# Seven-product chunks on places 0, 2, 4, 6 and 1, 3, 5 in the late stages of a hybrid encoder layer

## The chip, the cores and the metric

One core of one Trainium2 chip. The metric is the device time of one execution in microseconds (us). The matrix engine is called PE or TensorE below, VectorE is DVE, ScalarE is ACT, GpSimd is POOL, and SyncE (SP) issues the transfers.

## The reference

A sequence of S = 256 tokens of width D = 2048 goes through one layer of two mixer branches (an mLSTM branch `ya` and an RG-LRU branch `yb`) in float32. The part that matters here is its end:

```python
ya = jnp.einsum('bsw,wd->bsd', ya, w_branch_a)
yb = jnp.einsum('bsw,wd->bsd', yb, w_branch_b)
merged = sigmoid(ga_p) * ya + sigmoid(gb_p) * yb      # ga_p, gb_p: columns of rms_norm(x) @ w_in
return x + jnp.einsum('bsd,de->bse', merged, w_out)   # then a last RMS norm
```

So there are five products of a 256 x 2048 matrix by a 2048 x 2048 weight matrix at the end: with w_branch_b, with the gate columns for b, with those for a, with w_branch_a, and with w_out.

## The kernel before, in words

Each float32 operand is split into a high and a low part in the matrix engine's reduced format, and a product is three matmuls: high by high (L174), high by low (L176), low by high (L177). Weights arrive in chunks of 256 rows of k by 512 columns (one tile `raw` of 128 x 1024, 512 KB, one transfer by SP). ScalarE casts the chunk to its high part `whi` and VectorE subtracts to get the low part `wlo` (L140, L141 in `load_chunk`). Activations (`sHL`, `sC`, `sD`, `sA`, `sB`) stay in SBUF, already split.

The late stages run in this order: WB (w_branch_b), GB (the gate for b), GA (the gate for a), WA (w_branch_a), WO (w_out). WB, GB, GA and WA each call `pair` twice. One `pair` makes two blocks of 512 columns over all of k, in eight chunks of k for each block. A chunk of both blocks is done in one of two ways:

- `plain`: a transfer, a cast and a subtraction for each block, then 12 matmuls for each block, 24 in all, into the block's accumulator `acc` in PSUM.
- `products`: a scheme with seven products on the 2 x 2 arrangement of half chunks, 21 matmuls. VectorE first makes sums of weight halves: t1 by L199 and L200, t2 by L203 and L204. ScalarE casts four pieces (L180: `b`, then three `whi`) and VectorE subtracts four times (L181: `b` on 512 columns, three `wlo` on 1024). Four of the seven products go to four single PSUM banks `aux` (p1, p5, p7, p6), three into the accumulators. The scheme needs a *form* of the activations, a stationary operand that `make_form` prepares beforehand: six VectorE operations (L277, L280 to L283, L285; two on 512 columns, four on 128; the first is left out where the sum exists already) and one cast (L284).

`kqs` names the chunks that are done by `products`, `places` the positions 0 to 7 in the pair's order at which these stand. After the last of them, ScalarE copies p1 (L252) and VectorE combines the four banks (L253 to L256). The chunks that are left are plain, first those of block 0, then those of block 1; behind each block VectorE adds its accumulator to the result (L262), which frees the accumulator for the next pair. Then an epilogue follows: in GB a sigmoid (L956) and a multiplication into the result (L957), in GA a sigmoid (L965).

There are two accumulators, so a pair's first matmul into one waits for the L262 of the pair before. `raw` has six buffers, `whi` and `wlo` four each; `b` alternates between two tiles. A scheduler sets the order of each engine's instructions when the program is built. It prefers what stands under `urgent()`; on the chip each engine then works strictly in that order. Forms of the normalised input (`h`) for chunks 0 and 4 exist since earlier stages, in the tiles F0 and F4; four slots of one tile PT hold others. The table of the weights on the host follows `kqs`, since a chunk done by `products` needs its halves of two blocks together.

Of the kernel before, what the change touches and what calls it, by code (L numbers as in the profile page):

```python
# [10 lines left out]
F32R = mybir.dt.float32r  # L11
# [8 lines left out]
NB = 512  # L20
# [3 lines left out]
EPS = 1e-6  # L24
NEG = -1e30

S_WB, S_GB, S_GA, S_WA = [((0, 2, 4), (0, 2, 4))] * 4
S_OZ = (((4, 0), (2, 4)), ((4,), (1,)), ((4, 0), (2, 5)), ((4, 0), (0, 2)))
S_V = (((4,), (4,)), ((4,), (4,)))
S_WO = (0, 1, 2, 4)  # L30
L_WB, L_GB, L_GA, L_WA = ((0, 2, 4), (0, 2, 4)), ((0, 2, 4), (0, 2, 4)), ((0, 2, 4), (0, 2, 4)), ((0, 2, 4), (1, 3, 5))
L_WO = (0, 2, 4, 6)
H_FORMS = (4, 0)
PLAN = (dict(Y=('c0', '', '', 'c1',),
# [12 lines left out]
def f(ap):  # L47
    return ap.bitcast(F32)
# [3 lines left out]
def hybrid_encoder(ctx: ExitStack, tc: tile.TileContext, x, xt, pk, bif, fg, wg, wi, wr, wa, wb, wo, out):  # L52
# [12 lines left out]
    def name(n):  # L65
        uid[0] += 1
        return f"{n}_{uid[0]}"
# [4 lines left out]
    def sl(tag, dt=F32, cols=4096):  # L72
        return slot.tile([P, cols], dt, tag=tag, name=name("s" + tag))
# [41 lines left out]
    def drain():  # L115
        while queue or any(lanes):
            tick()
        lanes.clear()
# [149 lines left out]
    def halves(t, i):  # L268
        return t[:, i * 1024:i * 1024 + NB], t[:, i * 1024 + NB:(i + 1) * 1024]

    def make_form(fm, full=None, parts=None, temp=None):
        u = xp.rearrange("p a b -> p (a b)") if temp is None else temp
        if full is None:
            full = u[:, NB:2 * NB]
            hi, lo = parts
            v = full if len(hi.shape) == 2 else full.rearrange("p (k s) -> p k s", s=S)
            dve.tensor_add(v, f(hi), f(lo))  # L277
        a11, a21, a12, a22 = [full[:, i * P:(i + 1) * P] for i in range(4)]
        s1, s2, s3, s4 = [u[:, i * P:(i + 1) * P] for i in range(4)]
        dve.tensor_add(s1, a21, a22)  # L280
        dve.tensor_sub(s2, s1, a11)
        dve.tensor_sub(s3, a11, a21)
        dve.tensor_sub(s4, a12, s2)  # L283
        act.copy(fm[0], u[:, :NB])  # L284
        dve.tensor_sub(fm[1], u[:, :NB], f(fm[0]))  # L285
# [20 lines left out]
    def half_tr(src, half, after=None, turn=False):  # L306
        ps, both = acc_pair()
        for kq in range(4):
            tick()
            hi, lo = load_chunk(src[half * 4 + kq])  # L310
            tiles = [(kq * 4 + kk, m, kk * S + m * P) for kk in range(4) for m in range(2)]
            for high in (False, True) if turn and kq % 2 else (True, False):
                for k, m, o in tiles:
                    if high:
                        pe.matmul(ps[m], hi[:, o:o + P], hl_t[:, 2 * k * S:2 * (k + 1) * S],  # L315
                                  start=(k == 0), stop=(turn and k == KT - 1), skip_group_check=True)
                    else:
                        pe.matmul(ps[m][:, :S], lo[:, o:o + P], hhi(k * S, (k + 1) * S),  # L318
                                  start=False, stop=(not turn and k == KT - 1), skip_group_check=True)
            if after:  # L320
                after(kq)
        return both.rearrange("p (m q s) -> p m q s", m=2, q=2)

    def fold(dst, both):
        t = hp.tile([P, NB], F32, tag="fold", name=name("fold"), bufs=1)
        t3 = t.rearrange("p (m s) -> p m s", m=2)
        with urgent():
            act.copy(t3, both[:, :, 1, :])
            d3 = dst if len(dst.shape) == 3 else dst.rearrange("p (m s) -> p m s", m=2)
            dve.tensor_add(d3, both[:, :, 0, :], t3)  # L330
        return dst
# [458 lines left out]
    def h_parts(kq):  # L790
        h4 = hl_t[:, kq * 4 * S:(kq + 1) * 4 * S].rearrange("p (k q s) -> p k q s", q=2, s=S)
        return [h4[:, :, q, :] for q in range(2)]
# [97 lines left out]
    yah, yal = Cols([yas["h"]], 4096), Cols([yas["l"]], 4096)  # L890
    ybh, ybl = [], []
    fslot = {}
    fm_t = []

    def form(x, kq, i, **kw):
        fslot[x, kq] = halves(fm_t[0], i)
        make_form(fslot[x, kq], **kw)

    def h_form(kq, i):
        form("h", kq, i, parts=h_parts(kq))  # L900

    def ya_form(kq, i):
        form("a", kq, i, parts=[t(kq * NB, (kq + 1) * NB) for t in (yah, yal)])

    def forms(x):
        return {kq: v for (n, kq), v in fslot.items() if n == x}
# [3 lines left out]

    k_yb, k_h, k_ya = (sorted(set(sum(v, ()))) for v in (S_WB, S_GB + S_GA, S_WA))
    k_h = [kq for kq in k_h if kq not in hf]
    early = [lambda kq=kq, i=i: h_form(kq, i) for kq, i in zip(k_h, (3, 0, 1))]
    early += [lambda kq=kq, i=i: ya_form(kq, i) for kq, i in zip(k_ya[:1], (3, 0, 1)[len(early):])]

    for j in range(4):
        for i in range(2):
            both = half_tr(wi[BLK_ZB + j], i)
            if i == 0:
                zt = hp.tile([P, 2 * NB], F32, tag="zz" if j else "vhi", name=name("zt"))  # L920
                sg = hp.tile([P, 2 * NB], F32, tag="to" if j else "vlo", name=name("sg"))
            fold(zt[:, i * NB:(i + 1) * NB], both)
        act.activation(sg, zt, AF.Silu)
        dve.tensor_mul(sg, sg, hs[:, j * 1024:(j + 1) * 1024])
        ybh.append(sl(f"C{j}", F32R, 1024))
        ybl.append(sl(f"D{j}", F32R, 1024))
        act.copy(ybh[j], sg)
        dve.tensor_sub(ybl[j], sg, f(ybh[j]))
        if j == 0:
            fm_t.append(sl("PT", F32R))  # L930
        if j == 0:
            drain()
        for kq in (2 * j, 2 * j + 1):
            if kq in k_yb:
                form("b", kq, k_yb.index(kq), full=sg[:, (kq % 2) * NB:(kq % 2 + 1) * NB])
        if j == 1:
            early[0]()
    ybh, ybl = Cols(ybh, 1024), Cols(ybl, 1024)
    nb11 = [0]

# [6 lines left out]
    sgv = [sgb[:, j * 1024:(j + 1) * 1024] for j in range(4)]  # L947
    for p in range(2):
        pair((wb[2 * p], wb[2 * p + 1]), ybh, ybl, forms("b"), S_WB[p], sgv[2 * p:2 * p + 2], b11, lambda jj: None, None, L_WB[p])
    for fn in early[1:]:  # L950
        fn()
    for p in range(2):
        gb = [sl(f"D{2 * p + i}", F32, 1024) for i in range(2)]

        def epi_gb(jj, p=p, gb=gb):
            act.activation(gb[jj], gb[jj], AF.Sigmoid)  # L956
            dve.tensor_mul(sgv[2 * p + jj], sgv[2 * p + jj], gb[jj])  # L957

        pair((wi[BLK_GB + 2 * p], wi[BLK_GB + 2 * p + 1]), hhi, hlo, forms("h"), S_GB[p], gb, b11, epi_gb, None, L_GB[p])
    ga = []  # L960
    for p in range(2):
        ga += [sl(f"C{2 * p + i}", F32, 1024) for i in range(2)]
# [2 lines left out]
            act.activation(ga[2 * p + jj], ga[2 * p + jj], AF.Sigmoid)  # L965

        pair((wi[BLK_GA + 2 * p], wi[BLK_GA + 2 * p + 1]), hhi, hlo, forms("h"), S_GA[p], ga[2 * p:], b11, epi_ga, None, L_GA[p])
    for i, kq in enumerate(k_ya[1:]):
        ya_form(kq, 1 + i)

    m_t = sl("HL", F32R, 8192)
    mh, ml = Cols([m_t[:, :4096]], 4096), Cols([m_t[:, 4096:]], 4096)
# [157 lines left out]
```

## Time and profile before

| | |
|---|---|
| median of three runs | 1013.25 us (1013.14 to 1013.77) |
| span of the profiled execution | 1012.2 us; the page gives no other time for it |
| PE busy | 1003.0 us, 99% of the span |
| VectorE busy | 875.8 us, 87% |
| ScalarE busy | 628.6 us, 62% |
| WB / GB / GA / WA | 583.8 to 668.0 / 751.0 / 834.2 / 917.2 us |

Times are microseconds from the start of the span; a row of the timeline gives start, duration, engine, line, operation, output and inputs, and in brackets the idle time ahead of it with what ended it. PEld is the loading of stationary operands, which runs beside the matmuls. A matmul's recorded 0.39 us overlaps with the next one's; what counts is the distance from start to start.

### The profile page before, as it was taken

Reading aid. Unit: us, or ns where it says so; the run is one execution under the profiler, and the core shown is the slowest. Engines: PE = TensorE matmul, PEld = TensorE weight load, DVE = VectorE, ACT = ScalarE, POOL = GpSimd, SP = SyncE. Lnnn points to the kernel's source line nnn. Section 1 sums busy time; section 2 is a strip of 40 time slices with the busy share of each in tenths; the row PEclk is TensorE's granted clock in tenths of the full one; section 3 lists DMA queues with packets and bytes.
Section 4 is the critical chain, followed back from the end, with each engine's and each line's share of the span. In section 5 each row is a group of like instructions: output and inputs, shape, how many; then the busy total and the mean of one; then the engine's idle time right before and its main releaser. Section 6 shows DMA issues by size and latency. Waiting matters only on the chain.

```text
span 1012.2 us, 13718 instructions
## 1 busy us (share of the span) xinstructions
PE 1003.0 (99%) x5045; PEld 853.2 (84%) x5045; DVE 875.8 (87%) x1167; ACT 628.6 (62%) x825; POOL 18.6 (2%) x37
## 2 busy tenths in 40 slices
PE   9999999999999999999999999999999999999997
PEld 9888988888888888888888888888888888888886
DVE  6687898889769888997697888998898988999996
ACT  7546477756695786667955564655655656455562
POOL 1000000001001000000100000000000000000000
PEclk9999999999999999999999999999999999999999
DMA  9765446565555565657466466666566656568452
GB/s 349 263 208 157 160 153 198 173 213 197 167 190 167 177 197 184 210 167 227 146 199 208 155 208 188 212 212 201 187 216 200 219 177 212 184 217 336 161 200 83
DMA packets 56387, 199.32 MB, mean 197 GB/s; under 512 B 6400, under 2 KB 7424, under 8 KB 55936
## 3 DMA queue, kind: packets, MB, share of 16 engines
q1 hardware_dynamic: 55456, 197.13, 58.9%
q10 hardware_dynamic: 864, 1.32, 0.4%
q8 instruction: 39, 0.64, 0.3%
q14 instruction: 28, 0.23, 0.1%
HBM read 196.33 MB, written 2.10 MB: 196 GB/s over the span
## 4 chain that ended last, share of the span: by engine, by line
PE 97%; DVE 1%; DMA 1%; ACT 0%; issue 0%; ACTq 0%; SPq 0%; DVEq 0%
PE acc L176 17%; PE acc L177 17%; PE acc L174 17%; PE acc L315 16%; PE acc L318 8%; PE aux L176 3%; PE aux L174 3%; PE aux L177 3%; PE aux L855 1%; PE aux L721 1%; PE aux L720 1%; PE aux L719 1%; PE aux L1053 1%; PE aux L1052 1%; PE aux L1051 1%; PE acc L156 1%
## 5 line engine op out<-in xcount | busy, mean ns | idle before, releaser
L140 ACT CAST whi<-raw 128x1024 fp32r<-128x1024 f32 (+1 forms) x284 | 294.8, 1046 | 196.0 <-PE acc L177 99.7
L141 DVE TENSOR_TENSOR wlo<-raw,whi 128x1024 fp32r<-128x1024 f32 (+1 forms) x284 | 341.5, 1213 | 76.2 <-ACT whi L140 74.4
L176 PE MATMUL acc<-wlo,sHL 128*128 128x512 f32 x554 | 215.9, 390 | 0.0
L177 PE MATMUL acc<-whi,sHL 128*128 128x512 f32 x554 | 215.8, 390 | 0.0
L174 PE MATMUL acc<-whi,sHL 128*128 128x512 f32 x554 | 213.3, 390 | 0.0
L315 PE MATMUL acc<-sHL,whi 128*128 128x512 f32 x704 | 175.9, 393 | 0.0
L315 PEld LDWEIGHTS acc<-sHL,whi 128*128 128x128 f32 x704 | 127.4, 189 | 23.5
L174 PEld LDWEIGHTS acc<-whi,sHL 128*128 128x128 f32 x554 | 104.0, 188 | 21.2
L176 PEld LDWEIGHTS acc<-wlo,sHL 128*128 128x128 f32 x554 | 104.1, 188 | 21.0
L177 PEld LDWEIGHTS acc<-whi,sHL 128*128 128x128 f32 x554 | 104.0, 188 | 20.9
L318 PEld LDWEIGHTS acc<-sHL,wlo 128*128 128x128 f32 x704 | 95.3, 190 | 6.0
L180 ACT CAST whi<-t 128x1024 fp32r<-128x1024 f32 x70 | 73.5, 1051 | 42.9 <-PE acc L177 13.9
L318 PE MATMUL acc<-sHL,wlo 128*128 128x256 f32 x704 | 99.0, 283 | 0.0
L181 DVE TENSOR_TENSOR wlo<-t,whi 128x1024 fp32r<-128x1024 f32 x70 | 85.5, 1222 | 9.0 <-ACT whi L180 8.5
L180 ACT CAST whi<-raw 128x1024 fp32r<-128x1024 f32 x37 | 39.0, 1053 | 27.6 <-PE acc L177 16.9
L181 DVE TENSOR_TENSOR wlo<-raw,whi 128x1024 fp32r<-128x1024 f32 x37 | 45.2, 1222 | 8.7 <-ACT whi L180 8.7
L180 ACT CAST b<-raw 128x512 fp32r<-128x512 f32 x28 | 17.4, 621 | 39.2 <-DMA raw<-wi 16.5
L176 PE MATMUL acc<-wlo,sC 128*128 128x512 f32 x92 | 35.9, 390 | 0.4 <-DVE wlo L141 0.4
L176 PE MATMUL acc<-wlo,sA 128*128 128x512 f32 x92 | 36.0, 392 | 0.0
L177 PE MATMUL acc<-whi,sD 128*128 128x512 f32 x92 | 35.8, 389 | 0.0
L177 PE MATMUL acc<-whi,sB 128*128 128x512 f32 x92 | 35.8, 389 | 0.0
L174 PE MATMUL acc<-whi,sC 128*128 128x512 f32 x92 | 35.3, 389 | 0.0
(361 smaller groups left out, 1589.1 us busy)
## 6 DMA issues: line engine op xcount, KB each, us to landing
raw<-wi SPq DMA_DIRECT2D x254, 512.0 KB, 4.2
raw<-wb SPq DMA_DIRECT2D x32, 512.0 KB, 4.1
raw<-wa SPq DMA_DIRECT2D x32, 512.0 KB, 4.0
raw<-wo SPq DMA_DIRECT2D x32, 512.0 KB, 4.8
raw<-wr SPq DMA_DIRECT2D x8, 512.0 KB, 4.0
sB<-x SPq DMA_DIRECT2D x4, 512.0 KB, 7.7
sA<-x SPq DMA_DIRECT2D x1, 2048.0 KB, 7.9
sA<-xt SPq DMA_DIRECT2D x7, 256.0 KB, 6.7
```

Source lines behind the costliest of these rows:

```text
L140: last_copy[0] = act.copy(hi[:, r], raw[:, r]).ins
L141: last_sub[0] = dve.tensor_sub(lo[:, r], raw[:, r], f(hi[:, r])).ins
L156: pe.matmul(ps[tb], a, wl, start=False, stop=False)
L174: pe.matmul(ps, a, wh, start=id(ps) not in began, stop=False)
L176: pe.matmul(ps, a, wl, start=False, stop=False)
L177: pe.matmul(ps, b, wh, start=False, stop=stop)
L180: act.copy(hi, v)
L181: dve.tensor_sub(lo, v, f(hi))
L315: pe.matmul(ps[m], hi[:, o:o + P], hl_t[:, 2 * k * S:2 * (k + 1) * S], start=(k == 0), stop=(turn and k == KT - 1), skip_group_check=True)
L318: pe.matmul(ps[m][:, :S], lo[:, o:o + P], hhi(k * S, (k + 1) * S), start=False, stop=(not turn and k == KT - 1), skip_group_check=True)
L719: pe.matmul(dst, whi[:, o:o + P], xh[:, r], start=True, stop=False)
L720: pe.matmul(dst, whi[:, o:o + P], xl[:, r], start=False, stop=False)
```

## The change

The first pair of each of the four stages does chunks 0, 2, 4 and 6 by `products`, on places 0, 2, 4, 6 (before: chunks 0, 2, 4 on these places). The second pair does three, on places 1, 3, 5; before, that was so in WA only, and on 0, 2, 4 in the other three stages. The forms that this needs: one more for b (chunk 6, in the slot that an early form of h had), two of h (chunks 2 and 6) built after WB into slots 0 and 1, and four of a: two built one after each pair of GB into slots 2 and 3, two built after GA into the tiles F0 and F4.

```diff
-S_WB, S_GB, S_GA, S_WA = [((0, 2, 4), (0, 2, 4))] * 4
+S_WB, S_GB, S_GA, S_WA = [((0, 2, 4, 6), (0, 2, 4))] * 4
...
-L_WB, L_GB, L_GA, L_WA = ((0, 2, 4), (0, 2, 4)), ((0, 2, 4), (0, 2, 4)), ((0, 2, 4), (0, 2, 4)), ((0, 2, 4), (1, 3, 5))
+L_WB, L_GB, L_GA, L_WA = [((0, 2, 4, 6), (1, 3, 5))] * 4
...
-    early = [lambda kq=kq, i=i: h_form(kq, i) for kq, i in zip(k_h, (3, 0, 1))]
-    early += [lambda kq=kq, i=i: ya_form(kq, i) for kq, i in zip(k_ya[:1], (3, 0, 1)[len(early):])]
...
-        if j == 1:
-            early[0]()
...
-    for fn in early[1:]:
-        fn()
+    for i, kq in enumerate(k_h):
+        h_form(kq, i)
...
         pair((wi[BLK_GB + 2 * p], ...), hhi, hlo, forms("h"), S_GB[p], gb, b11, epi_gb, None, L_GB[p])
+        ya_form(k_ya[p], 2 + p)
...
-    for i, kq in enumerate(k_ya[1:]):
-        ya_form(kq, 1 + i)
+    for kq, slot_ in zip(k_ya[2:], H_FORMS[::-1]):
+        fslot["a", kq] = halves(sl(f"F{slot_}", F32R, 1024), 0)
+        make_form(fslot["a", kq], parts=[t(kq * NB, (kq + 1) * NB) for t in (yah, yal)])
```

Later lines move up by three to five: the sigmoid of GB is L951 after the change and its multiplication L952, the sigmoid of GA L961. In the instruction counts PE goes from 5030 to 5018 rows (L174, L176 and L177 lose four each), VectorE from 1151 to 1192, ScalarE from 814 to 825; SP's transfers stay at 387.

Below are rows of the orders. A row gives the line, the operation, its output and its inputs, with buffer numbers. `t` are the sums of weight halves, `b11` is b, `sD0` and `sD1` hold the gate blocks, `aux` the four banks.

VectorE before the change, in GB between the first and the second pair, from the last combination of the banks (L256) to the first `wlo` of the second pair's first product chunk:

```order
L256 TENSOR_TENSOR sD1_1341_6228<-aux_1357_6257,sD0_1340_6227 128x512
L199 TENSOR_TENSOR t_1435_6575<-raw_1432_6568 128x512
L181 TENSOR_TENSOR b11_1434_6572<-raw_1432_6568,b11_1434_6572 128x512
L200 TENSOR_TENSOR t_1435_6575<-raw_1433_6569,raw_1432_6568 128x512
L141 TENSOR_TENSOR wlo_1421_6527<-raw_1419_6525,whi_1420_6526 128x1024
L141 TENSOR_TENSOR wlo_1425_6545<-raw_1423_6543,whi_1424_6544 128x1024
L203 TENSOR_TENSOR t_1436_6576<-t_1435_6575,raw_1432_6568 128x512
L262 TENSOR_TENSOR sD0_1340_6227<-sD0_1340_6227,acc_1342_6229 128x1024
L181 TENSOR_TENSOR wlo_1438_6580<-t_1435_6575,whi_1437_6579 128x1024
```

Two subtractions for plain chunks (L141) and the first accumulator's L262 stand among the work for the second pair, and three more plain chunks of each block come behind L253 on PE.

VectorE after the change, at the same turn, from the first combination (L253) to the second product chunk's `b`:

```order
L253 TENSOR_TENSOR sD1_1345_6244<-aux_1363_6275,sD0_1344_6243 128x512
L141 TENSOR_TENSOR wlo_1433_6571<-raw_1431_6569,whi_1432_6570 128x1024
L141 TENSOR_TENSOR wlo_1442_6603<-raw_1440_6601,whi_1441_6602 128x1024
L200 TENSOR_TENSOR t_1451_6644<-raw_1449_6638,raw_1448_6637 128x512
L254 TENSOR_TENSOR sD0_1344_6243<-aux_1362_6274,sD1_1345_6244 128x512
L141 TENSOR_TENSOR wlo_1446_6621<-raw_1444_6619,whi_1445_6620 128x1024
L203 TENSOR_TENSOR t_1452_6645<-t_1451_6644,raw_1448_6637 128x512
L255 TENSOR_TENSOR sD1_1345_6244<-aux_1361_6273,sD1_1345_6244 128x512
L256 TENSOR_TENSOR sD1_1345_6244<-aux_1361_6273,sD0_1344_6243 128x512
L181 TENSOR_TENSOR wlo_1454_6649<-t_1451_6644,whi_1453_6648 128x1024
L204 TENSOR_TENSOR t_1452_6645<-raw_1449_6638,t_1452_6645 128x512
L181 TENSOR_TENSOR b11_1474_6727<-raw_1472_6723,b11_1474_6727 128x512
```

The four combinations now alternate with the last plain chunk's subtractions (1433), with those of the second pair's place 0 (1442, 1446) and with the sums of its place 1 (L200, L203, L204). The rows that follow directly:

```order
L262 TENSOR_TENSOR sD0_1344_6243<-sD0_1344_6243,acc_1346_6245 128x1024
L262 TENSOR_TENSOR sD1_1345_6244<-sD1_1345_6244,acc_1347_6246 128x1024
L199 TENSOR_TENSOR t_1475_6730<-raw_1472_6723 128x512
L200 TENSOR_TENSOR t_1475_6730<-raw_1473_6724,raw_1472_6723 128x512
L181 TENSOR_TENSOR wlo_1456_6655<-t_1452_6645,whi_1455_6654 128x1024
L181 TENSOR_TENSOR wlo_1458_6659<-raw_1449_6638,whi_1457_6658 128x1024
L952 TENSOR_TENSOR sE_1169_5556<-sE_1169_5556,sD0_1344_6243 128x1024
L952 TENSOR_TENSOR sE_1169_5556<-sE_1169_5556,sD1_1345_6244 128x1024
L203 TENSOR_TENSOR t_1476_6731<-t_1475_6730,raw_1472_6723 128x512
L141 TENSOR_TENSOR wlo_1466_6689<-raw_1464_6687,whi_1465_6688 128x1024
```

Both L262 stand here, behind `wlo_1454` and `b11_1474`, and the two multiplications L952 stand ahead of `wlo_1466`, a plain chunk of the second pair.

PE after the change, at the same turn, beginning 35 rows behind the last matmul into p6 (`aux_1363`, which L253 reads); between them stand the rest of that product chunk, one plain chunk of each block and the second pair's first `b` product:

```order
L174 MATMUL aux_1461_6664<-whi_1453_6648,sF0_295_1520 128x512
L174 MATMUL aux_1459_6662<-b11_1474_6727,sHL_5_90 128x512
L174 MATMUL aux_1460_6663<-whi_1453_6648,sF0_295_1520 128x512
L176 MATMUL aux_1460_6663<-wlo_1454_6649,sF0_295_1520 128x512
L177 MATMUL aux_1460_6663<-whi_1453_6648,sF0_295_1520 128x512
L176 MATMUL aux_1461_6664<-wlo_1454_6649,sF0_295_1520 128x512
L177 MATMUL aux_1461_6664<-whi_1453_6648,sF0_295_1520 128x512
L176 MATMUL aux_1459_6662<-b11_1474_6727,sHL_5_90 128x512
L177 MATMUL aux_1459_6662<-b11_1474_6727,sHL_5_90 128x512
L174 MATMUL aux_1462_6665<-whi_1455_6654,sF0_295_1520 128x512
L174 MATMUL acc_1437_6599<-whi_1441_6602,sHL_5_90 128x512
```

The last row is the first matmul into an accumulator of the second pair; it needs the first L262 above. `wlo_1466` is first used 39 rows further on.

ScalarE after the change, at the same turn in GA:

```order
L140 CAST whi_1623_7309<-raw_1622_7308 128x1024
L180 CAST whi_1631_7337<-t_1629_7333 128x1024
L180 CAST b11_1652_7416<-raw_1650_7412 128x512
L180 CAST whi_1633_7343<-t_1630_7334 128x1024
L961 ACTIVATE sC0_1522_6941<-sC0_1522_6941 128x1024
L180 CAST whi_1635_7347<-raw_1627_7327 128x1024
```

The cast of `b11_1652`, which belongs to the product chunk on the second pair's place 3, stands ahead of `whi_1633`, which belongs to the one on place 1; `raw_1650` is the sixth transfer after `raw_1618` and takes its buffer.

## Prediction

> **What bounds the kernel now.** I read the page first (shares, chain of waits), then the busy time by stage, then the waits. The page gives no time for the profiled execution beside its span of 1012.2 us; the median of the three runs is 1013.25 us, so I set 1.05 us around the span and make every sum against 1013.25.
>
> ```profile
> PE 1003.0 (99%) x5045; PEld 853.2 (84%) x5045; DVE 875.8 (87%) x1167; ACT 628.6 (62%) x825; POOL 18.6 (2%) x37
> ...
> PE 97%; DVE 1%; DMA 1%; ACT 0%; issue 0%; ACTq 0%; SPq 0%; DVEq 0%
> ```
>
> TensorE is busy 99% of the span and carries 97% of the chain. So a matmul less is time saved, as long as nothing makes TensorE wait. The four stages that the change touches (WB, GB, GA, WA) run from 583.8 to 917.2 us. Their first, their last and their sum (columns: stretch, its length, busy time of PE, PEld, DVE, ACT, POOL, granted clock, DMA share, GB/s):
>
> ```profile
> 583.80:668.00 84.20, 83.83 (x370) 69.04 (x369) 76.73 (x94) 47.76 (x54) 0.00 (x0) 1.00 0.63 206
> ...
> 834.20:917.20 83.00, 83.00 (x375) 68.71 (x374) 75.82 (x86) 45.91 (x49) 0.00 (x0) 1.00 0.63 214
> sum 333.40, PE 333.03 PEld 275.34 DVE 301.67 ACT 189.45 POOL 0.00; mean PE 83.26 PEld 68.84 DVE 75.42 ACT 47.36 POOL 0.00
> ```
>
> There TensorE is busy 333.03 of 333.40 us at full clock, and VectorE already 301.67, 90%. Who waits there (us in total, times, longest), from 583 to 940 us:
>
> ```profile
> ACT b L180 <- DMA raw<-wi: 16.5, 11, 2.7
> DVE wlo L141 <- ACT whi L140: 12.6, 12, 1.7
> DVE wlo L181 <- ACT whi L180: 12.3, 15, 1.7
> ...
> PE acc L176 <- DVE wlo L141: 0.4, 1, 0.4
> ```
>
> TensorE waited once, 0.4 us. The cover is good now; the question is whether it survives.
>
> **What the change saves.** A chunk moved from the plain form (24 matmuls) to seven products (21) drops three; four chunks drop 12. Their pitch, start to start over 17 steps:
>
> ```profile
> 668.05 0.39 PE L174 MATMUL aux<-whi,sF 128*128 128x512 f32 x1
> ...
> 671.90 0.39 PE L177 MATMUL acc<-whi,sHL 128*128 128x512 f32 x1
> ```
>
> (671.90 - 668.05) / 17 = 0.2265 us, so 12 matmuls are worth 2.72 us, all on the path. The number of SP's transfers stays.
>
> **What it adds on VectorE.** Pitches of operations on 512, 1024 and 128 columns:
>
> ```profile
> 696.53 0.68 DVE L256 TENSOR_TENSOR sD<-aux,sD 128x512 f32<-128x512 f32 x1
> 697.13 0.69 DVE L199 TENSOR_TENSOR t<-raw 128x512 f32<-128x512 f32 x1
> ...
> 698.93 2.36 DVE L141 TENSOR_TENSOR wlo<-raw,whi 128x1024 fp32r<-128x1024 f32 x2
> 701.20 0.69 DVE L203 TENSOR_TENSOR t<-t,raw 128x512 f32<-128x512 f32 x1
> 701.80 1.22 DVE L262 TENSOR_TENSOR sD<-sD,acc 128x1024 f32<-128x1024 f32 x1
> 702.94 1.22 DVE L181 TENSOR_TENSOR wlo<-t,whi 128x1024 fp32r<-128x1024 f32 x1
> ```
> ```profile
> 646.71 0.28 DVE L280 TENSOR_TENSOR xp<-xp 128x128 f32<-128x128 f32 x1
> 646.91 0.29 DVE L282 TENSOR_TENSOR xp<-xp 128x128 f32<-128x128 f32 x1
> ```
>
> 512 columns take 0.60 us (697.13 - 696.53), 1024 columns 1.135 (two in 701.20 - 698.93), 128 columns 0.20. A product chunk is five of the first and three of the second, 6.4 us; a chunk in plain form two of the second, 2.27. Four chunks add 16.6 us. Three more forms in these stages add two 512-column and four 128-column operations each, 2.0 us, 6.0 in all (the form for b adds less than that in the stage ahead, where the order keeps it off the path). VectorE's load becomes 301.7 + 22.6 = 324.3 us of the 330.7 that TensorE now needs: 98%. ScalarE gains two casts a chunk and three for forms, some 9 us on 189 of 333; idle time hides them, except where told below.
>
> **Where the cover goes.** With products on places 0, 2, 4, 6, one plain chunk of each block (24 matmuls) stands after the last product, where three of each (72) stood. In the trace, the last product's final matmul in GB's first pair (aux p6, the matmul that L253 needs) and the next pair's first product lie 19.3 us apart; in the new order it is 35 rows, 7.93 us:
>
> ```profile
> 690.26 0.39 PE L177 MATMUL aux<-whi,sF 128*128 128x512 f32 x1
> ...
> 709.53 0.39 PE L174 MATMUL aux<-whi,sF 128*128 128x512 f32 x1
> ```
>
> In that gap VectorE works in series, as the rows of the new order show for GB: L253, then twelve more to the end of the first L262, which frees the accumulator that the next pair's first plain matmul writes. That is eight of 0.602 and five of 1.135, 10.49 us, and 0.12 for the last one's tail and hand-over. When does L253 start? Two pairs of rows bound it:
>
> ```profile
> 607.05 0.39 PE L177 MATMUL aux<-whi,sPT 128*128 128x512 f32 x1
> ...
> 607.90 0.69 DVE L253 TENSOR_TENSOR sE<-aux,sE 128x512 f32<-128x512 f32 x1 [0.56 <-PE acc L177]
> ```
> ```profile
> 690.94 0.39 PE L177 MATMUL acc<-whi,sHL 128*128 128x512 f32 x1
> ...
> 691.37 1.06 ACT L140 CAST whi<-raw 128x1024 fp32r<-128x1024 f32 x1 [0.26 <-PE acc L177]
> ```
>
> The only L253 that waited started 0.85 us after the start of p6's last matmul; ScalarE shows the quickest hand-over from TensorE, 0.43 (I use 0.45). So, with p6's last matmul at zero, L262 ends at 11.06 to 11.46. TensorE reaches the matmul that needs it after 45 rows, at 10.20: it waits 0.86 to 1.26 us. WB's rows there are of the same kinds in the same order: 0.86 to 1.26 again. In WA the chain has one 512-column operation less (9.89) and 43 rows of room (9.75): 0.71 to 1.11. GA has the same 9.89 and 44 rows (9.97), but another wait ends later. Its b11_1652 comes in a raw buffer that is freed by wlo_1620, the fifth of the chain, at 4.65 to 5.05.
>
> ```profile
> 691.44 0.33 SPq L190 DMA_DIRECT2D raw<-wi  x1
> ```
> ```profile
> 695.03 0.62 ACT L180 CAST b<-raw 128x512 fp32r<-128x512 f32 x1 [1.24 <-DMA raw<-wi]
> ...
> 704.60 1.28 ACT L956 ACT_TABLE_LOAD   x1
> 705.89 1.06 ACT L956 ACTIVATE sD<-sD 128x1024 f32<-128x1024 f32 x1
> 706.86 1.03 ACT L180 CAST whi<-t 128x1024 fp32r<-128x1024 f32 x1
> ```
>
> From issue to cast of b took 3.59 us (I use 3.7). So b is cast from 8.35, and whi_1633, next on ScalarE, is done at 8.35 + 0.62 + 1.06 = 10.03; TensorE wants it after 39 rows, at 8.84: 1.2 to 1.6 us. GB has a second place. There ScalarE casts whi_1457 when its buffer's former tile, whi_1441, is done with (12.70 + 0.86 + 0.43 = 14.0); the table load and both sigmoids follow: 14.0 + 1.06 + 1.28 + 0.97 + 1.06 = 18.4. In VectorE's order both L952 stand ahead of wlo_1466: the second can start at 18.55, L203 follows, and wlo_1466 is there at 21.5. TensorE wants it after 84 rows, at 19.04 + 0.86 = 19.9. Another 1.6 us.
>
> [...]
>
> Before the change, the same counting sets that accumulator free 8.7 us ahead of its use, so no such wait was seen. At the turns from a second pair to the next stage two chunks of each block follow the last product, and 3 us of room stay; I cost them at nothing, with VectorE's last 2% as the only cover. The forms that are built later than before stand chunks ahead of their first product and cost nothing but VectorE's time.
>
> Sum of waits: WB 0.86 to 1.26, GB 2.5 to 2.9, GA 1.2 to 1.6, WA 0.71 to 1.11; 5.3 to 6.9. I take the middle, 6.1, since one pair of rows speaks for each end. 1013.25 - 2.72 + 6.1 = 1016.6 us.
>
> **Rivals.**
> Accumulator waits only: the transfer in GA lands sooner and GB's sigmoids hold nothing up. Then 0.86 + 0.86 + 0.49 + 0.71 = 2.9, or 4.5 with the slow hand-over: 1013.4 to 1015.1 us, no change to speak of. For it: b's cast waits for its transfer 1.5 us a time now and TensorE never felt it. Against: the order of rows.
>
> Faster: the vector operations behind p6 get through sooner than their pitches say. It decides where L262 ends before 10.20 (WB, GB), 9.97 and 9.75, that is with 0.5 to 0.9 us off a chain of some 10 us even at the quick hand-over. Then only the matmuls count, 1010.5 us. For it: no chain so tight ran before, and some of its rows may stand earlier than I count. Against: no row has 512 columns under 0.60.
>
> VectorE bounds all through: its idle time, 333.4 - 301.7 = 31.7 us, is mostly waits for casts, which wait for buffers. If half stays, the stages take 324.3 + 15.9 = 340.2, 6.8 us more than now: 1020.0.
>
> Full durations: each operation in the chains takes its recorded time, 0.69 or 1.22, as it waits on the one ahead: 8 x 0.09 + 5 x 0.085 = 1.1 us more a place, 4.5 in all, 1021.1. [...] The trace agrees with the durations, not with such a pitch.
>
> That fewer matmuls are not issued at all is out: the new order has 5018 PE rows against 5030.
>
> **How the numbers follow.** I count within 0.2% (2.03 us) as no change, about what measuring this kernel can tell. Forecast, 1015.3 to 1018.5: 0.55. Accumulator waits only: 0.18. Faster: 0.10. VectorE the bound: 0.13; full durations: 0.04. So slower 0.55 + 0.13 + 0.04 = 0.72, same 0.18, faster 0.10. The range leaves out the faster case and the full durations: 1011.8 to 1020.6.
>
> **What would show it.** After the change TensorE should show waits that it did not have: for L262 at the start of the second pairs' accumulators in WB, GB and WA, for a cast (L180) in GA, and for wlo (L141) shortly after the sigmoids in GB; each 0.7 to 1.7 us. VectorE's busy time in the four stages should be near 324 us. I am wrong if these waits are under 3 us together, or if they stand at the turns between stages.

## The result: 1030.19 us, 1.6% slower

The changed kernel takes 1030.19 us (median of four runs, 1027.39 to 1033.82) against 1013.19 for the kernel before (1013.10 to 1013.77): ratio 1.0164, 95% interval 1.0139 to 1.0189. Forecast were 1016.6 us and a range up to 1020.6. The sign was right, the size was not: 17.0 us lost and 2.7 us of matmuls not gained make 19.7 us of new waiting, where 6.1 had been counted.

The page after, shares and chain of waits (profiled execution: span 1027.3 us, 1029.06 us in all):

```profile
PE 1009.0 (98%) x5033; PEld 852.2 (83%) x5033; DVE 896.8 (87%) x1208; ACT 633.6 (62%) x836; POOL 19.5 (2%) x37
...
PE 79%; DVE 10%; DMA 6%; issue 3%; ACT 2%; ACTq 0%; DVEq 0%; SPq 0%
```

The chain was 97% TensorE; now 18% of it runs through VectorE, transfers and ScalarE. The waits from 560 to 960 us:

```profile
ACT b L180 <- DMA raw<-wi: 33.4, 12, 4.5
...
ACT whi L180 <- DVE t L204: 16.9, 8, 4.8
...
PEld aux L174 <- ACT b L180: 9.3, 5, 3.7
...
PE aux L174 <- ACT b L180: 7.6, 4, 3.3
```

TensorE waits for casts of b, and these for their transfers (the first line; `raw` is the tile that a transfer fills). Comparing the start of each 512-column matmul with the one before plus the pitch of 0.2267 us gives the time lost in each stage, waits and slow matmuls together:

| stage | before | after | forecast of new waits |
|---|---|---|---|
| WB | 0.7 us | 5.4 us | 0.86 to 1.26 |
| GB (with the turn from WB) | 0.0 | 7.0 | 2.5 to 2.9 |
| GA | 0.0 | 2.8 | 1.2 to 1.6 |
| WA | 0.5 | 2.0 | 0.71 to 1.1 |
| WO | 0.3 | 1.2 | none |

That is 16.9 us more; less 2.7 for the matmuls it makes 14.2 of the 15.1 us by which the span grew. Of the rest, 0.4 us comes before WB.

The turn in WB shows the mechanism, engine by engine. TensorE: p6's last matmul, the first one that waited, and three later ones:

```profile
617.68 0.39 PE L177 MATMUL aux<-whi,sPT 128*128 128x512 f32 x1
...
629.49 0.50 PE L174 MATMUL aux<-b,sC 128*128 128x512 f32 x1 [3.29 <-ACT b L180]
...
631.28 0.63 PE L176 MATMUL aux<-b,sC 128*128 128x512 f32 x1
631.70 0.63 PE L177 MATMUL aux<-b,sD 128*128 128x512 f32 x1
632.13 0.63 PE L174 MATMUL aux<-whi,sPT 128*128 128x512 f32 x1
```

VectorE, with L253, which p6 allows:

```profile
615.32 1.22 DVE L181 TENSOR_TENSOR wlo<-raw,whi 128x1024 fp32r<-128x1024 f32 x1
617.89 0.69 DVE L199 TENSOR_TENSOR t<-raw 128x512 f32<-128x512 f32 x1 [1.35 <-DMA raw<-wb]
618.50 0.69 DVE L181 TENSOR_TENSOR b<-raw,b 128x512 fp32r<-128x512 f32 x1
619.42 1.23 DVE L141 TENSOR_TENSOR wlo<-raw,whi 128x1024 fp32r<-128x1024 f32 x1 [0.24 <-ACT whi L140]
620.57 0.68 DVE L253 TENSOR_TENSOR sE<-aux,sE 128x512 f32<-128x512 f32 x1
...
622.90 1.22 DVE L141 TENSOR_TENSOR wlo<-raw,whi 128x1024 fp32r<-128x1024 f32 x1
```

SP's queue, and ScalarE's cast of b:

```profile
612.41 0.33 SPq L190 DMA_DIRECT2D raw<-wb  x1
...
624.15 0.33 SPq L190 DMA_DIRECT2D raw<-wb  x1
```
```profile
628.82 0.62 ACT L180 CAST b<-raw 128x512 fp32r<-128x512 f32 x1 [4.20 <-DMA raw<-wb]
```

L253 started 2.89 us after p6's last matmul, since three rows stand ahead of it and the first, L199, waited for the second pair's first transfer, which took 5.5 us (612.41 to 617.89). The subtraction that frees a raw buffer ended at 624.12; SP issued b's transfer at 624.15, ScalarE cast b 4.67 us later, and TensorE had stood still for 3.29 us. Soon after that its matmuls come every 0.43 us instead of 0.23. The same by stretches (columns as in the prediction; the granted clock is the third from the end):

```profile
625.00:629.40 4.40, 1.21 (x6) 0.67 (x4) 4.39 (x6) 0.58 (x1) 0.00 (x0) 1.00 0.93 286
629.40:634.00 4.60, 4.51 (x13) 3.55 (x14) 4.53 (x6) 2.14 (x3) 0.00 (x0) 0.64 0.29 117
634.00:640.00 6.00, 6.00 (x28) 4.99 (x27) 4.33 (x5) 1.92 (x2) 0.00 (x0) 1.00 0.53 178
```

So that wait cost another 1.7 us through a lower granted clock: 0.64 is the mean of the second stretch, and from 630.7 to 634.0 us it was 0.50.

### The profile page after: what moved, and what is told of

It is laid out like the page before. It is cut to its first block, busy times and chain, and to the rows that moved or that the text cites. A ratio compares the mean times of both kernels' runs of the same rounds, so it can differ in the third digit from the quotient of the medians.

```text
span 1027.3 us, 13760 instructions
## 1 busy us (share of the span) xinstructions
PE 1009.0 (98%) x5033; PEld 852.2 (83%) x5033; DVE 896.8 (87%) x1208; ACT 633.6 (62%) x836; POOL 19.5 (2%) x37
## 4 chain that ended last, share of the span: by engine, by line
PE 79%; DVE 10%; DMA 6%; issue 3%; ACT 2%; ACTq 0%; DVEq 0%; SPq 0%
PE acc L315 16%; PE acc L176 12%; PE acc L174 12%; PE acc L177 12%; PE acc L318 8%; DMA raw<-wi 4%; DVE wlo L141 3%; PE aux L176 2%; PE aux L174 2%; PE aux L177 2%; DVE wlo L181 2%; DMA raw<-wb 1%; ACT whi L140 1%; PE aux L855 1%; PE aux L721 1%
## 5 line engine op out<-in xcount | busy, mean ns | idle before, releaser
L141 DVE TENSOR_TENSOR wlo<-raw,whi 128x1024 fp32r<-128x1024 f32 (+1 forms) x276 | 332.4, 1212 | 71.8 <-ACT whi L140 70.2
L140 ACT CAST whi<-raw 128x1024 fp32r<-128x1024 f32 (+1 forms) x276 | 285.1, 1045 | 164.5 <-PE acc L177 75.0
L176 PE MATMUL acc<-wlo,sHL 128*128 128x512 f32 x542 | 211.9, 391 | 0.0
L177 PE MATMUL acc<-whi,sHL 128*128 128x512 f32 x542 | 211.2, 390 | 0.0
L174 PE MATMUL acc<-whi,sHL 128*128 128x512 f32 x542 | 208.2, 390 | 0.0
L180 ACT CAST whi<-t 128x1024 fp32r<-128x1024 f32 x78 | 82.0, 1052 | 65.6 <-PE acc L177 28.4
L176 PEld LDWEIGHTS acc<-wlo,sHL 128*128 128x128 f32 x542 | 101.9, 188 | 22.0 <-DVE wlo L141 0.9
L174 PEld LDWEIGHTS acc<-whi,sHL 128*128 128x128 f32 x542 | 101.9, 188 | 21.3 <-DVE xp L330 0.4
L177 PEld LDWEIGHTS acc<-whi,sHL 128*128 128x128 f32 x542 | 101.9, 188 | 20.5
L181 DVE TENSOR_TENSOR wlo<-t,whi 128x1024 fp32r<-128x1024 f32 x78 | 94.9, 1219 | 6.1 <-ACT whi L180 5.9
L180 ACT CAST b<-raw 128x512 fp32r<-128x512 f32 x32 | 19.8, 621 | 62.6 <-DMA raw<-wi 33.4
L180 ACT CAST whi<-raw 128x1024 fp32r<-128x1024 f32 x41 | 43.1, 1050 | 19.9 <-PE acc L177 9.1
L181 DVE TENSOR_TENSOR wlo<-raw,whi 128x1024 fp32r<-128x1024 f32 x41 | 50.0, 1219 | 3.6 <-ACT whi L180 3.6
L199 DVE TENSOR_TENSOR t<-raw 128x512 f32<-128x512 f32 x37 | 25.4, 687 | 10.3 <-DMA raw<-wi 4.9
L176 PE MATMUL acc<-wlo,sA 128*128 128x512 f32 x86 | 33.8, 393 | 0.0
L176 PE MATMUL acc<-wlo,sC 128*128 128x512 f32 x86 | 33.8, 393 | 0.0
L177 PE MATMUL acc<-whi,sD 128*128 128x512 f32 x86 | 33.7, 392 | 0.0
L177 PE MATMUL acc<-whi,sB 128*128 128x512 f32 x86 | 33.6, 391 | 0.0
```

The lines of the kernel that those rows point to most:

```text
L140: last_copy[0] = act.copy(hi[:, r], raw[:, r]).ins
L141: last_sub[0] = dve.tensor_sub(lo[:, r], raw[:, r], f(hi[:, r])).ins
L174: pe.matmul(ps, a, wh, start=id(ps) not in began, stop=False)
L176: pe.matmul(ps, a, wl, start=False, stop=False)
L177: pe.matmul(ps, b, wh, start=False, stop=stop)
L180: act.copy(hi, v)
```

## The experiments

Runs of one group share a chip and the runs of the kernel before. Unless told otherwise, an edit is made to the changed kernel.

**Buffers and places.** e1_raw7:

```diff
-raw = wp.tile(..., tag="raw", bufs=6)
+raw = wp.tile(..., tag="raw", bufs=7)      # and gn moved into another tile
```

> The changed kernel with seven raw buffers in place of six (a 128-byte helper tile, gn, moves into another tile to make room). Theory T (the b of the second pair's place 3 comes late: its transfer may only start when a VectorE subtraction behind L253 frees a raw buffer, and then takes about 4.7 us): the buffer is free one chunk sooner, 1.1 to 1.7 us, at each turn, so TensorE's waits for b, now 3.3, 2.6, 0.95 and 0.8 us, fall to about 2, 1.5, 0 and 0 and the slow matmuls behind the long ones become fewer: 1019 to 1024 us. Rival V (VectorE's load of 98% is the bound): buffers change nothing, 1027 to 1034. Rival A (the accumulators freed by L262, as predicted): nothing either, 1027 or more.

Measured 1025.56 us (ratio to before 1.0117, 95% interval 1.0099 to 1.0136; below, the numbers in brackets are the same two). One buffer gave back 4.6 us, less than theory T had it and more than V and A. In its profile the waits at the turns of GA and WA are gone, those in WB and GB are shorter, and behind them the predicted wait for the accumulator comes to light:

```profile
628.79 0.50 PE L174 MATMUL aux<-b,sC 128*128 128x512 f32 x1 [0.73 <-ACT b L180]
...
634.43 0.47 PE L174 MATMUL acc<-whi,sC 128*128 128x512 f32 x1 [1.70 <-DVE sE L262]
```

The buffers are a part of the cause, not all.

e2_sec235, second pairs on 2, 3, 5:

> The changed kernel with the second pairs' three product chunks on places 2, 3, 5 in place of 1, 3, 5: same matmuls, same VectorE work, but one plain chunk more of each block (5.4 us of TensorE) between a first pair's last product and the second pair's first. T: the waits at the four turns go, 1010.5 to 1015. V: same load, 1027 to 1034. A: the accumulator is still needed as early by the plain chunk on place 0, so its 2.9 to 4.5 us would stay: 1013.4 to 1016.

Measured 1035.34 us (1.0212, 1.0197 to 1.0227), above all three ranges: theory T failed here, and V and A named no time as long. Room for b does not help when the plain chunk on place 0 needs the accumulator; in WA its wait alone was 3.30 us:

```profile
894.95 0.47 PE L174 MATMUL acc<-whi,sA 128*128 128x512 f32 x1 [3.30 <-DVE sD L262]
```

e3_before135, the kernel before with its second pairs on 1, 3, 5:

> The kernel before with its second pairs' products on places 1, 3, 5 in all four stages; the first pairs keep three products on 0, 2, 4. T: after place 4 three plain chunks of each block remain, so no wait: 1012.8 to 1013.8. V: 297 to 302 us of VectorE work as before: no change either. Rival P (the second pair's places are at fault, not the fourth product): 1020 or more.

Measured 1017.88 us (1.0037, 1.0024 to 1.0050), four us more, where T had none and rival P at least six. By the count above it loses 5.3 us in the five stages where the kernel before loses 1.5, spread over all of them; no single wait of TensorE in the late stages is longer than 0.5 us.

e4_p0235, first pairs on 0, 2, 3, 5:

> The changed kernel with the first pairs' four products on places 0, 2, 3, 5 in place of 0, 2, 4, 6: same matmuls and VectorE work, two plain chunks of each block (48 matmuls, 10.9 us) after the last product. T: the turns have 5.4 us more room, waits there go: 1010.5 to 1014, perhaps with small waits between places 2 and 3, where two product chunks follow each other. V: 1027 to 1034.

Measured 1021.82 us (1.0071, 1.0054 to 1.0088). One more plain chunk of room gives back 8.4 us of the 19.7, but 11.3 us are still missing to 1010.5. Both theories were off.

**VectorE's load.** e5_before_load, the kernel before with useless work (the rows shortened):

```diff
                 split(h3, l3, r2)
+                u = xp.rearrange("p a b -> p (a b)")[:, :2 * NB]
+                dve.tensor_add(u, u, f(l3))          # in WB, GB, GA, WA only
```

> The kernel before, with one useless VectorE operation on 1024 columns behind each of the 24 product chunks of WB, GB, GA and WA (its result is used by nothing): VectorE's load there rises by 24 x 1.135 = 27.2 us to 329 of 333 us, as high as with the change or higher, while places, buffers and transfers stay. Theory T2 (the loss sits at the turns: one plain chunk of room; VectorE is held in its order by a transfer and frees raw buffers late): load alone is mostly harmless with three plain chunks of room, 1013 to 1017. Rival V (VectorE's load is the bound): 1024 to 1034.

Measured 1024.11 us (1.0105, 1.0090 to 1.0120). As rival V had it, load costs 10.7 us at the old places and with three plain chunks of room. Its load, 329 us by count, is 5 us above the change's 324. In its profile 2.17 us of this is one wait at the change from WA to WO, the others are below 1.1 us each.

e6_pool_t1:

```diff
-                dve.tensor_sub(t1[:, :2], v1[:, 2:], v1[:, :2])
-                dve.tensor_sub(t1[:, 2:], v2[:, :2], v1[:, 2:])
+                sub = dve if sums else pool
+                sub.tensor_sub(t1[:, :2], v1[:, 2:], v1[:, :2])
+                sub.tensor_sub(t1[:, 2:], v2[:, :2], v1[:, 2:])
```

> The changed kernel with the two t1 sums of each product chunk (L199, L200) on GpSimd in place of VectorE. What GpSimd needs for one of these no row of the late stages shows. T2: VectorE no longer waits in its order for the second pair's first transfer, so L253 starts sooner after p6 and the raw buffer for b is freed sooner; the waits at the turns fall by half, 1018 to 1024. V: 28 us less on VectorE in the four stages (89% load), so the loss goes: 1010.5 to 1014. Either fails if GpSimd is slow, then 1030 and more.

Measured 1052.14 us (1.0380, 1.0359 to 1.0401): GpSimd is slow. Groups of GpSimd and of VectorE from 583 to 917 us (count, then busy time and mean ns of one, then idle time ahead):

```profile
L200 POOL TENSOR_TENSOR t<-raw 128x512 f32<-128x512 f32 x25 | 53.0, 2122 | 200.0 <-DVE wlo L181 103.7 <-DMA raw<-wi 49.6 <-DMA raw<-wa 27.0
L201 POOL TENSOR_TENSOR t<-raw,raw 128x512 f32<-128x512 f32 x26 | 46.7, 1795 | 28.0 <-DMA raw<-wa 12.6 <-DMA raw<-wi 12.3 <-DMA raw<-wb 3.0
```
```profile
L181 DVE TENSOR_TENSOR b<-raw,b 128x512 fp32r<-128x512 f32 x27 | 28.9, 1071 | 15.2 <-ACT b L180 15.1
```

The run says nothing of theory T2 or V.

e7_light, the sums of chunk 6 left out:

> The changed kernel with the four sums (L199, L200, L203, L204) of every product chunk 6 left out, its pieces cast straight from raw; that part of the computation is missing. VectorE loses 5 x 4 x 0.60 = 12 us (WO has one such chunk too), its load in the four stages falls from 98% to 95%. T2: the turn itself is unchanged, L253 still stands behind the second pair's L199: 1025 to 1031. V: half of the added load is gone, so at least half of the loss: 1016 to 1022.

Measured 1031.97 us (1.0175, 1.0138 to 1.0213; its runs lie between 1025.63 and 1035.03). No gain, against V; T2's range is missed at its upper end.

e8_halves, r1 in two transfers, b's half first:

> The changed kernel with each product chunk's first transfer (r1) in two halves, the half that b needs first. T2: b is cast about 1 us sooner at each turn, so TensorE's waits for b shrink from 3.3, 2.6, 0.95 and 0.8 us by about 1 us each, and the slow matmuls behind the two long ones become fewer: 1023 to 1028. V: no change, 1027 to 1034.

Measured 1028.48 us (1.0148, 1.0131 to 1.0165), 1.7 us below the change, whose runs it overlaps, and 0.5 above T2's range. Its trace says more than its time: at the turns of WB, GB, GA and WA TensorE waited 1.66, 1.79, 0.59 and 1.42 us for b, three of the four less than in the change, and yet by the count above the five stages lose 18.8 us where the change loses 18.4. The loss moved to other places, among them waits of 0.91 us for a `wlo` in GA and of 0.68 us for a cast in WA. So the wait for b's transfer does not set the time by itself.

**The seventh buffer again.** e9_gawa_raw7, only GA and WA changed, seven buffers:

> Only GA and WA as the change has them (four products on 0, 2, 4, 6, three on 1, 3, 5), WB and GB as before, and seven raw buffers as in e1_raw7. Six matmuls fewer than before, 1.36 us. Theory T3 (loss by a loop: VectorE's queue frees raw buffers late, their transfers land late, VectorE and ScalarE wait for them; one buffer more opens it where VectorE has no forms and multiplications beside): e1's profile shows next to no waits in these two stages, so 1011.8 to 1012.8 us. Rival V (VectorE's load of 98% alone costs some 10 us over four stages, 5 over two): 1015 to 1019.

e11_before_raw7, the control:

> The kernel before with seven raw buffers (and the helper tile moved), the control for the others: the matrix engine waits 0.4 us in all of these stages now, so no change by any theory, 1012.5 to 1013.8.

Measured e9 1015.23 us (1.0013, 1.0004 to 1.0022) and e11 1015.63 (1.0018, 1.0010 to 1.0027). The control was not neutral: seven buffers cost the kernel before 2.0 us. Its profile shows nothing lost from WB to GA, but by the same count 1.2 us between 400 us and WB, where the kernel before loses none; that was not followed further. Taken as it stands, e9 lies in V's range and above T3's. Against e11, e9 is 0.4 us faster, of 1.36 due: two stages with the change and seven buffers roughly break even, which is nearer to T3.

e10_raw7_p0245, first pairs on 0, 2, 4, 5 with seven buffers:

> Seven raw buffers, all four stages with four products, but the first pairs' products on places 0, 2, 4, 5 (two plain chunks of each block behind the last), the second pairs' on 1, 3, 5. T3: room and buffer together, 1011 to 1016. V: 1020 or more.

Measured 1018.50 us (1.0047, 1.0034 to 1.0061), between the two expectations, neither of which held.

e12_load_raw7, the useless work with seven buffers:

> e5_before_load (before, with 24 useless VectorE operations) with seven raw buffers. T3: the load hurts by holding raw buffers, so one more buffer gives back at least half of its 10.7 us: 1014 to 1018. V: the load itself is the cost, 1022 to 1025.

Measured 1023.54 us (1.0099, 1.0085 to 1.0112), 7.9 above its control e11. So the load's cost does not come from raw buffers for the greater part: T3 fails, V's range holds.

**Load and room, crossed.** e13_light_all leaves all four sums out of the product chunks of the four stages; e14_p0235_light does so with room:

```diff
+                light = not sums and late[0]
+                if light:
+                    t1, t2 = v1, v2
+                else:
                     dve.tensor_sub(t1[:, :2], v1[:, 2:], v1[:, :2])
...
-L_WB, L_GB, L_GA, L_WA = [((0, 2, 4, 6), (1, 3, 5))] * 4
+L_WB, L_GB, L_GA, L_WA = [((0, 2, 3, 5), (1, 3, 5))] * 4   # e14 only
```

> The changed kernel with the four sums (L199, L200, L203, L204) of all product chunks in WB, GB, GA and WA left out, pieces cast straight from raw; that part of the computation is missing. VectorE loses 28 x 4 x 0.60 = 67 us there: load 78% in place of 98%, and fewer steps from raw to the casts; places, transfers and buffers as changed. Theory V (the load is the cause): 1010.5 to 1013. Theory R (the room at the turns): the turn still has L253 behind the second pair's b and the accumulators behind L253, so 1016 to 1022.

> e13_light_all with the first pairs' products on places 0, 2, 3, 5 (room behind the last product as in e4_p0235). V: 1010.5 to 1013 too. R: here as well 1010.5 to 1013. If neither, and 1015 or more, the second pairs' places 1, 3, 5 are what is left (4 us in e3_before135).

Measured e13 1015.19 us (1.0015, 1.0006 to 1.0024) and e14 1011.14 (0.9975, 0.9966 to 0.9984). e13 lies between V's range and R's, e14 within both. With e4 and the change:

| | VectorE full | sums left out |
|---|---|---|
| one plain chunk behind the last product | 1030.19 | 1015.19 (e13) |
| two | 1021.82 (e4) | 1011.14 (e14) |

e14 stands 0.6 us from 1010.5, what the kernel before would take with 12 matmuls less: room and a light VectorE together remove the whole loss, and the second pairs' places cost nothing then. Short room alone costs 4.1 us, VectorE's sums alone 10.7, both together 19.1 (each run against the kernel before in its own group: 4.1, 10.5 and 19.6). TensorE's longest wait at each of e13's four turns is for b (L180 to L181 are L182 to L183 in e13 and e14, L174 to L177 are L176 to L179):

```profile
626.10 0.50 PE L176 MATMUL aux<-b,sC 128*128 128x512 f32 x1 [0.19 <-ACT b L182]
...
709.01 0.50 PE L176 MATMUL aux<-b,sHL 128*128 128x512 f32 x1 [0.34 <-ACT b L182]
...
792.31 0.50 PE L176 MATMUL aux<-b,sHL 128*128 128x512 f32 x1 [0.68 <-ACT b L182]
...
875.68 0.50 PE L176 MATMUL aux<-b,sA 128*128 128x512 f32 x1 [0.80 <-ACT b L182]
```

What ScalarE waits for from 583 to 917 us shows the other side. In e4:

```profile
ACT whi L180 <- DVE t L204: 36.5, 14, 4.6
ACT whi L140 <- PE acc L177: 24.0, 21, 2.1
```

In e14:

```profile
ACT whi L140 <- PE acc L179: 44.7, 35, 2.6
ACT whi L182 <- PE acc L179: 40.8, 37, 2.3
```

With the sums, casts wait for VectorE's t2 (L204); without them there is no L204 to wait for, and they wait for TensorE to free buffers. The kernel before, which has these sums and whose TensorE is busy 99% of the span, looks like e14 in this: over the same stretch

```profile
ACT whi L140 <- PE acc L177: 48.5, 38, 2.5
...
ACT whi L180 <- DVE t L204: 3.9, 4, 2.6
```

e15_sec024, second pairs back on 0, 2, 4:

> The changed kernel with the second pairs' products back on places 0, 2, 4. R: the second pair's first product now follows the first pair's one plain chunk at once and needs its sums 5.4 us sooner: worse than the change, 1035 to 1045. Theory P (the places 1, 3, 5 are at fault, as e3_before135's 4 us hint): 1024 to 1028.

Measured 1030.19 us (1.0165, 1.0151 to 1.0179), the same as the change, so neither R's nor P's number. That the totals agree is chance, for the waits are others: by the count above WB loses 9.3 us and GA 0.8, where the change loses 5.4 and 2.8, and the long waits in WB and GB are now the predicted ones, for the accumulator:

```profile
635.03 0.77 PE L174 MATMUL acc<-whi,sC 128*128 128x512 f32 x1 [3.13 <-DVE sE L262]
...
724.40 0.47 PE L174 MATMUL acc<-whi,sHL 128*128 128x512 f32 x1 [3.13 <-DVE sD L262]
```

The second pairs' places decide which wait comes last at a turn; here they did not change the sum.

e16_gawa_p0245, the candidate:

> A candidate: WB and GB as before; GA and WA with four products in their first pairs, on places 0, 2, 4, 5, second pairs as before (0, 2, 4 in GA; 1, 3, 5 in WA). Six matmuls fewer, 1.36 us. With VectorE at 95% (GA) and 98% (WA) of the time there, V says a loss of 2 to 5 us: 1014 to 1018. R: room is there, 1011.8 to 1013.

Measured 1015.54 us (1.0018, 1.0009 to 1.0027). V was right; it does not beat the kernel before.

**Middle loads.** e17_p0235_light6 leaves out the sums of chunk 6 only, e18_p0235_noforms the six late forms, both with room:

> e4_p0235 (four products on 0, 2, 3, 5, three on 1, 3, 5) with the four sums of the product chunks 6 left out as in e7_light; that part of the computation is missing. VectorE's load 95% with room. V (load): between e14's 1011.1 and e4's 1021.8, near 1016 to 1019. If the load is no matter of degree, as e7_light suggests: 1020 to 1023.

> e4_p0235 with the six forms that are built in the late stages (two of h, four of a) left out and older tiles used in their places; that part of the computation is missing. VectorE's work drops by 12 us, 5.1 of it in GB, where the work between the ends of WB and GB comes down from 83.2 to 78.1 us (TensorE needs 82.3). V by stage: GB's loss, 6.1 us in e4's profile, goes below 2 us, WB's too: 1014 to 1017. If only the total counts, as in e17: 1016 to 1019.

Measured e17 1020.54 us (1.0070, 1.0055 to 1.0085) and e18 1019.00 (1.0055, 1.0038 to 1.0072). Some 12 us less VectorE work give 1.3 and 2.8 us against e4 (0.6 and 2.2 with each run set against the kernel before in its own group). In e18's profile GB's loss falls from 6.1 to 2.5 us, which was the sense of it, but WB keeps its 2.2. e17 is where it was expected if the load is no matter of degree, e18 at the upper end of what counts the total alone. The cost is not proportional to the load.

## Why the prediction was wrong

The rows on which the sum rested, at the four turns between a first and a second pair of the changed kernel (us):

| turn | p6's last matmul to L253 | SP's issue to the cast of b | TensorE's wait for b |
|---|---|---|---|
| counted | 0.45 to 0.85 | 3.7 (in GA only) | none |
| WB | 2.89 | 4.67 | 3.29 |
| GB | 2.51 | 4.74 | 2.57 |
| GA | 1.66 | 3.75 | 0.95 |
| WA | 0.84 | 3.80 | 0.79 |

- *TensorE bounds, and 12 matmuls are worth 2.72 us.* Right: e14, with no loss left in it, ran 2.6 us under the kernel before of its group.
- *L253 starts 0.45 to 0.85 us after p6's last matmul.* This step failed first. It held in WA alone; L253 came up to 2.0 us later than the upper bound. The bounds came from rows where VectorE had nothing else to do; the order's rows ahead of L253 (L199 on a fresh transfer, b, a plain chunk's subtraction) were taken as done.
- *From issue to cast of b, 3.7 us.* Right in GA and WA, 1 us short in WB and GB. The graver error is that only GA's turn was given a transfer for b at all: the wait for b was the longest at all four. GA's three waits there (0.26, 0.95 and 0.45 us) and WA's 0.79 are near the counted 1.2 to 1.6 and 0.71 to 1.11, but only GA's 0.45 is a wait that was counted (for the cast of `whi`): the rest of the likeness is luck.
- *The accumulator's wait.* Real, but covered: b came later still. It shows in e1 (1.70 us), e2 (3.30) and e15 (3.13, twice).
- *GB's second place, wlo behind L952.* Not there: no wait of TensorE stands at that point in GB.
- *The other turns cost nothing.* Failed: 2.5 us at the start of GB's first pair, from 672.5 to 690 us (waits of 0.29, 0.68 and 0.45 us in TensorE's rows, the last 15 us behind the turn, and slow starts around them; operations of the forms of h stand among VectorE's rows there, and in e18, which leaves the forms out, GB lost less).
- *The clock* had no term. Behind the two long waits the matmuls at up to 0.43 us cost 1.7 us each time.
- *The signs.* VectorE's busy time was near 324 us as forecast: 325.5 of the 347.8 us from 583.8 to 931.6. Of the waits that were named only the cast in GA came, 0.45 us, so by its own test (under 3 us together) the mechanism was wrong.
- *VectorE at 98% of the four stages* was a mean over unlike stages. Adding the pitches of the new order's rows, VectorE's work between the ends of WB and GB is 82.0 us where TensorE needs 82.3; before, it was 73.3. GB lost most in the change and in e1, e2 and e4, and e18 took work out of GB and gained there. But this is not the whole account: WA has 81.1 us of such work and lost only 2.0, and in e15 WB lost most. The rival *VectorE bounds all through* got 0.13 and 1020.0 us; VectorE stood idle 22.3 us in these stages, where the rival kept 15.9. e5 shows that load on VectorE can cost 10.7 us without any change of room, and the crossed runs that the sums and the short room together cost more than the two taken singly.

Not settled: leaving out the sums takes away load (to 78%, less than the 90% before the change) and also two steps between a transfer and its cast, and the runs do not part the two. e5 speaks for load, e7, e17 and e18 against load as a plain quantity. Nor is it settled what e3's places cost 4 us by.

## What to carry to other kernels

Where one engine is at 90% and feeds the bound one, count its work stage by stage before adding any: a mean of 98% hid a stage with 82.0 us of work for 82.3. When a serial chain on such an engine is timed, start it at the end of what stands ahead of it in its queue, not at the event that allows it, and count the buffers that its late rows hold back from transfers. A saving on the bound engine is only worth having if the work left behind the last expensive piece still covers a transfer and that chain; here room alone was not enough (e4, 1021.82 us), the second engine needed slack as well (e14, 1011.14 us). And a wait that goes away in the trace is no gain until the time says so: in e8 and e15 the loss only moved.

## What the hardware showed

- Behind TensorE's idle times of 3.29 and 2.57 us its granted clock fell to 0.50 (from 630.7 to 634.0 us and from 719.5 to 722.7; 0.64 and 0.62 in the mean over some 4.5 us), with matmuls 0.427 us apart; after the 0.95 us wait in GA it stayed at 1.00. It also fell to 0.50 in e4 behind a wait of 1.78 us (684.5 to 687.7), but not in e1 behind one of 1.70 (632 to 637 us), while in e1's GB it did behind waits of 1.24 and 0.45 us close together (718.9 to 722.0). So in these runs no single length of wait decides it.
- In e6 a 512-column subtraction took 1.8 to 2.1 us on GpSimd by the profile's rows (0.69 on VectorE), and VectorE's subtraction for b grew from 0.69 to 1.07 us in the mean.
- The spread from run to run (longest less shortest) was 0.6% for the change and 0.9% for e7, four runs each. The kernel before spread over 0.07% in four runs and 0.35% in 21 beside e9; e15, as slow as the change, over 0.1% in four. So a kernel whose TensorE waits can spread more, but need not.
